# Decoder layer on one core: the third quarter of the output projection for all tokens ahead of the fourth, the triangle matrix kept in another tile, and the slot positions of three token groups taken later

## The chip, the core and the metric

The kernel runs on one core of a Trainium2 chip. A core has five engines with a queue of instructions each: TensorE (PE in the rows: matmuls; PEld its weight loads), VectorE (DVE), ScalarE (ACT), GpSimd (POOL) and SyncE (SP), which here issues every transfer from and to the chip's memory. An engine takes its instructions in the order of its queue and waits at the first one whose inputs or whose place are not ready. The metric is the time of one execution on the device in microseconds (us); less is better.

## What is computed

One layer of a decoder on 512 tokens of 1024 numbers, all in float32 (shapes in the comments):

```python
mixed = sigmoid(ga) * (o_a @ w_proj_a) + sigmoid(gb) * (o_b @ w_proj_b)   # two attention branches
x = x + mixed @ w_out                                                     # [512,1024] @ [1024,1024]
x = x + hier_moe(rms_norm(x, g_ffn), ...)                                 # 32 experts, 2 per token
return rms_norm(x, g_final)

def hier_moe(h, ...):
    g_logit = xt @ w_group + b_group                  # best of 4 groups
    e_logit = (xt @ w_expert + b_expert)              # best 2 of the group's 8 experts
    gate = g_w * top_p / sum(top_p)
    ...
    hid = silu(xb @ w1[e]) * (xb @ w3[e]); return hid @ w2[e]   # 1024 -> 512 -> 1024
```

The change lies between the second line and the first expert: output projection, RMSNorm, choice of experts (routing), and gathering the tokens of each expert.

## The kernel before, in words

The tokens are worked on in NT = 4 groups t of 128. The output projection is cut into four quarters n of 256 columns; `x2_chunk(n, t)` multiplies group t of the merged branches (tile `mt[t]`) with quarter n of the weights (pair `ws[n]`, high and low float32r part) in 24 matmuls (L703 to L705) and adds the result to x on DVE (L707). A table `seq` sets the order of the sixteen chunks. After each, `turn(n, t)` transposes the new columns (PE L733), copies them out of PSUM into the tile `misc` (ACT L736) and sums their squares (ACT L738); for n = 3 that gives the group's scale `rs2` (DVE L744, POOL L745). `logits(n, t)` adds the chunk's share of the routing logits (PE L751).

When a group's four quarters are there, four functions follow for it:

- `route(t)`: some eleven small DVE operations, L758 to L775: logits to `lg`, best group, best two experts, ending in a 0/1 matrix `E[t]`.
- `place(t)`: a matmul of E with the strict triangle `tri` (PE L781; for odd t also L783) counts how many earlier tokens chose the same expert; DVE writes the slot number (`pos`, L784) and the 0/1 gather matrix `sel` (`one_hot`, L826).
- `gates(t)`: eight small DVE operations (L793 to L805) and two on ACT: the gate weights G.
- `h2_parts(t)`: the normalised tokens as float16 high and low parts (tile `h2`): ACT L812 and L817, then a subtraction on POOL (L818) for both halves of the columns; for t = 2 and 3 the second half is subtracted on DVE (L814).

`gather(xs, sel, h, a)` (PE L834, L835; DVE L839) then builds the experts' inputs from h2 and sel: half h = 0 needs groups 0 and 1, h = 1 groups 2 and 3. The experts follow in 8 rounds of 4, each with 24 pieces of weights of 1 MB; `up` and `down` use a piece (PE L886, L893), and `use` gives its place free after the last matmul on it.

Places: SBUF is cut into 22 slots of one piece each (class `Slots`). x2 takes two of them, h2 two, the routing weights with the triangle one (`early`); `mt[t]`, `ws[n]` hold others until they are done. `fetch(n)` takes n free slots and issues the transfer of the next n pieces on SP (L623), which waits there, with everything behind it, until the slot's last user is done. When all that is free, 18 pieces fit; the nineteenth goes out when `use` has freed the first one. For that, five pieces are first multiplied for h = 0 alone (AHEAD = 5), and the first is free after its h = 1 half.

The order of each queue comes from a scheduler at build time, except where `manual_schedule` keeps the order of the code: SP from L691 on, PE and DVE from the last chunk on (`in_order`, in the loop over `seq`), until L1029.

Of the kernel before, what the change touches and what calls it, by code (L numbers as in the profile page):

```python
# [10 lines left out]
F32 = mybir.dt.float32  # L11
# [10 lines left out]
P = 128  # L22
# [10 lines left out]
NL = 40  # L33
# [104 lines left out]
def layer_kernel(ctx: ExitStack, tc: tile.TileContext, xT, x, w_ki, w_ch, w_ab, w_out, g_mix, g_ffnk, g_fin, w_r, b_r,  # L138
# [20 lines left out]
    def t2(shape, dtype=F32, name="t2", tag="r"):  # L159
        return temps[tag][0].tile(shape, dtype, tag=tag, name=name, bufs=temps[tag][1])  # L160
# [451 lines left out]
    def fetch(n):  # L612
        for _ in range(n):
            if not todo or not S.idle:
                return
            if todo[0] == (NQ - 1, PIECES - 4) and not gfn:
                gfn.append(S.get([P, D], F32, "gfn"))
                sp.dma_start(out=gfn[0], in_=g_fin)
                if not S.idle:
                    return  # L620
            q, i = todo.pop(0)
            have[q, i] = S.get([P, QE * FF], F32, "we")
            sp.dma_start(out=have[q, i], in_=w_e[q, i])  # L623
# [9 lines left out]
    br = cp.tile([P, NL], F32, name="br")  # L633
    gfk = cp.tile([P, NK], F32, name="gfk")
    gf8 = cp.tile([P, NK], F32, name="gf8")
    early = S.get([P, NK * NL + P], F32, "early")
    wr, tri = early[:, :NK * NL].rearrange("p (k c) -> p k c", k=NK), early[:, NK * NL:]
    for dst, src in ((br, b_r), (gfk, g_ffnk), (wr, w_r), (tri, const[:, C_COLS["tri"][0]:])):
        sp.dma_start(out=dst, in_=src)
    dve.tensor_scalar(gf8, gfk, 1.0 / H2, None, ALU.mult)  # L640
    merging = ExitStack()
# [48 lines left out]
    S.add(ctx.enter_context(tc.tile_pool(name="more1", bufs=1, side="right", reuse_waits="tile")), N_RIGHT, "m1")  # L690
    ordered = ExitStack()  # L691
    ordered.enter_context(tc.manual_schedule(engines={mybir.EngineType.SP}))
    misc = t2([P, 4 * P], name="misc", tag="y")

    def x2_chunk(n, t, between={}):

        hi, lo = ws[n]
        ps = bank()[:, :CW]
        for k in range(NK):
            for f, *args in between.get(k, ()):  # L700
                f(*args)
            a = mt[t][:, 0, k]
            pe.matmul(ps, a, hi[:, k], start=k == 0, stop=False)  # L703
            pe.matmul(ps, a, lo[:, k], start=False, stop=False)  # L704
            pe.matmul(ps, mt[t][:, 1, k], hi[:, k], start=False, stop=k == NK - 1)  # L705
        o = x2t(t)[:, n * CW:(n + 1) * CW]
        dve.tensor_tensor(o, ps, o, ALU.add)  # L707
# [14 lines left out]
    dve.memset(zero, 0.0)  # L722
    pe.matmul(lps[:, :NT * NL], ident, zero, start=True, stop=False, skip_group_check=True)

    seq = [(n, t) for n in range(2) for t in range(NT)] + [(n, t) for t in range(NT) for n in (2, 3)]
    xts = {}

    def turn(n, t):

        xc = x2t(t)[:, n * CW:(n + 1) * CW]  # L730
        tr = pa.tile([P, 512], F32, tag="sc", name="xtr")
        for k in range(2):
            pe.transpose(tr[:, k * P:(k + 1) * P], xc[:, k * P:(k + 1) * P], ident)  # L733
        a = 2 * P * (seq.index((n, t)) % 2)
        xs = xts[n, t] = misc[:, a:a + 2 * P].rearrange("p (k q) -> p k q", k=2)
        act.copy(xs, tr[:, :CW].rearrange("p (k q) -> p k q", k=2))  # L736
        junk = t2([P, CW], name="junk", tag="hT")
        act.activation(junk, xc, AF.Square, accum_out=ssp[:, t, n:n + 1])  # L738
        if n == 2:
            dve.tensor_reduce(pre[:, t:t + 1], ssp[:, t, 0:3], AX.X, ALU.add)  # L740
            dve.tensor_scalar(pre[:, t:t + 1], pre[:, t:t + 1], 1.0 / (D * H2 * H2), EPS / (H2 * H2), ALU.mult, ALU.add)
        if n == 3:
            r = rs2[:, t:t + 1]
            dve.scalar_tensor_tensor(r, ssp[:, t, 3:4], 1.0 / (D * H2 * H2), pre[:, t:t + 1], ALU.mult, ALU.add)  # L744
            pool.tensor_tensor(r, r, half[:, 0:1], ALU.pow)  # L745
# [102 lines left out]

    sel = t2([P, NT, QE, CAP], F16, name="sel", tag="sel")
    for n, t in seq:  # L850
        if n == 2 and t % 2 == 0:
            h2.append(S.get([P, 2, 2, NK, P], F16, "h2"))
            fetch(len(S.idle))
        if (n, t) == seq[-1]:

            in_order.enter_context(tc.manual_schedule(engines={mybir.EngineType.PE, mybir.EngineType.DVE}))
            x2_chunk(n, t, {3: [(turn, n - 1, t)], 6: [(logits, n - 1, t)]})
        else:
            x2_chunk(n, t)
        if n < 2 and t == NT - 1:  # L860
            S.free(*ws[n])
            fetch(2 - n)
        if n == 3:
            S.free(mt[t])
            if t % 2 == 0:
                fetch(1)
        if (n, t) not in seq[-2:]:
            turn(n, t)
            logits(n, t)
            if n == 3:  # L870
                route(t)
                place(t)
                gates(t)
                h2_parts(t)
        if n == 2 and t == NT - 1:
            S.free(*ws[2])
            fetch(2)
    S.free(*ws[3])
    xs = t2([P, NK, 2, P], name="xs", tag="xs")

# [130 lines left out]

    gather(xs, sel, 0, 0)
    turn(3, NT - 1)
    gather(xs, sel, 0, 4)
    logits(3, NT - 1)
    route(NT - 1)

    h1 = two(pa, "sc", "h1")
    for k in range(AHEAD):
        up(0, k, (0,), h1, xs, have[0, k])  # L1020
        if k == AHEAD - 2:
            h2_parts(NT - 1)
            place(NT - 1)
            S.free(early)
    for a in (0, 4):
        gather(xs, sel, 1, a)
    gates(NT - 1)
    in_order.close()
    fetch(len(S.idle))  # L1029
# [171 lines left out]
```

## Time and profile before

| | |
|---|---|
| time, median of 3 runs | 920.62 us (920.29 to 921.29) |
| profiled execution, its time | 922.1 us |
| its span in the trace | 920.2 us |
| PE busy | 870.4 us (95%) |
| DVE busy | 401.3 us (44%) |
| ACT, POOL busy | 273.2 us (30%), 210.5 us (23%) |
| moved by DMA | 244.50 MB, mean 266 GB/s |
| granted PE clock, mean | 0.994 of full speed |

The span runs from the first to the last instruction in the trace; the time of an execution is 1.9 us longer. Shares are means over stages: the first 440 us or so are attention and projections, the rest the experts. Times in rows count from the span's start. A group's name is its source line, engine and operation; buffer numbers are left out of tile names, so that x2 reads `x`, rs2 `rs`, ev `ev` or `e`.

### The profile page before, as it was taken

Reading aid. Unit: us, or ns where it says so; the run is one execution under the profiler, and the core shown is the slowest. Engines: PE = TensorE matmul, PEld = TensorE weight load, DVE = VectorE, ACT = ScalarE, POOL = GpSimd, SP = SyncE. Lnnn points to the kernel's source line nnn. Section 1 sums busy time; section 2 is a strip of 40 time slices with the busy share of each in tenths; the row PEclk is TensorE's granted clock in tenths of the full one; section 3 lists DMA queues with packets and bytes.
Section 4 is the critical chain, followed back from the end, with each engine's and each line's share of the span. In section 5 each row is a group of like instructions: output and inputs, shape, how many; then the busy total and the mean of one; then the engine's idle time right before and its main releaser. Section 6 shows DMA issues by size and latency. Waiting matters only on the chain.

```text
span 920.2 us, 15647 instructions
## 1 busy us (share of the span) xinstructions
PE 870.4 (95%) x6444; PEld 516.3 (56%) x6444; DVE 401.3 (44%) x957; ACT 273.2 (30%) x582; POOL 210.5 (23%) x135
## 2 busy tenths in 40 slices
PE   7998999999999999999999999999989989989894
PEld 5898779678777877899734243433323214232221
DVE  4736799994444444732814123131311303313113
ACT  5556664562444554534401001010100000101012
POOL 2597445452315831612100000000000000000003
PEclk9999999999999999999999999999999999999998
DMA  9422102112215221682799999999999999999993
GB/s 334 143 70 93 66 27 92 63 53 69 71 69 194 80 92 49 213 360 98 306 410 420 420 421 420 421 419 422 418 421 419 421 420 420 421 419 420 421 403 129
DMA packets 40685, 244.50 MB, mean 266 GB/s; under 512 B 4896, under 2 KB 5280, under 8 KB 16032
## 3 DMA queue, kind: packets, MB, share of 16 engines
q1 hardware_dynamic: 40608, 243.45, 66.5%
q8 instruction: 52, 0.85, 0.4%
q14 instruction: 25, 0.20, 0.1%
HBM read 241.33 MB, written 2.10 MB: 265 GB/s over the span
## 4 chain that ended last, share of the span: by engine, by line
PE 61%; DMA 27%; DVE 6%; POOL 2%; ACT 2%; issue 1%; SPq 0%; POOLq 0%; ACTq 0%
DMA we<-in_w_e_dram 26%; PE h L886 9%; PE y L893 9%; PE mm L264 5%; PE mm L266 5%; PE mm L265 5%; PE ops L475 2%; PE mm L704 2%; PE mm L703 2%; PE mm L705 2%; PE mm L520 2%; PE mm L519 2%; PE mm L518 2%; PE mm L349 2%; PE mm L351 2%; PE mm L350 2%
## 5 line engine op out<-in xcount | busy, mean ns | idle before, releaser
L886 PE MATMUL h<-we,xs 128*32 128x512 f32 x2048 | 237.5, 596 | 20.8 <-DMA we<-in_w_e_dram 20.2
L886 PEld LDWEIGHTS h<-we,xs 128*32 128x32 f32 x2048 | 57.8, 109 | 173.0 <-issue 103.3
L171 POOL TENSOR_TENSOR wl<-raw,wh 128x1024 fp32r<-128x1024 f32 (+1 forms) x41 | 97.1, 2389 | 111.1 <-ACT wh L170 55.6
L893 PE MATMUL y<-we,hT 128*32 128x512 f32 x1024 | 115.4, 595 | 1.6 <-DMA we<-in_w_e_dram 1.4
L264 PE MATMUL mm<-xh,wh 128*128 128x512 f32 (+1 forms) x272 | 109.0, 401 | 0.5 <-DVE bias L408 0.5
L1100 POOL TENSOR_TENSOR fo<-x,gfn 128x512 f32<-128x512 f32 x4 | 5.0, 1287 | 443.4 <-DMA we<-in_w_e_dram 442.6
L266 PE MATMUL mm<-xh,wl 128*128 128x512 f32 (+1 forms) x272 | 106.2, 390 | 0.1
L265 PE MATMUL mm<-xl,wh 128*128 128x512 f32 (+1 forms) x272 | 105.7, 389 | 0.0
L953 DVE TENSOR_TENSOR x<-cps,x 128x512 f32<-128x512 f32 x60 | 41.2, 689 | 91.2 <-PE cps L951 91.0
L893 PEld LDWEIGHTS y<-we,hT 128*32 128x32 f32 x1024 | 30.5, 109 | 71.7 <-issue 59.3
L927 DVE SCALAR_TENSOR_TENSOR silu<-silu,gate,h 128x512 f32<-128x512 f32 x16 | 12.0, 747 | 118.8 <-PE h L886 117.8
L266 PEld LDWEIGHTS mm<-xh,wl 128*128 128x128 f32 x272 | 51.4, 189 | 11.1 <-DVE wl L171 0.6
L264 PEld LDWEIGHTS mm<-xh,wh 128*128 128x128 f32 x272 | 51.5, 189 | 10.0 <-issue 1.0
L170 ACT CAST wh<-raw 128x1024 fp32r<-128x1024 f32 (+1 forms) x46 | 45.6, 1027 | 35.5 <-DMA raw<-in_w_ch_dram 13.2
L265 PEld LDWEIGHTS mm<-xl,wh 128*128 128x128 f32 x272 | 51.6, 190 | 8.0
L934 ACT COPY hT<-htr 128x512 f32<-128x512 f32 x16 | 8.6, 589 | 151.9 <-PE htr L932 151.9
L170 ACT CAST y<-y 128x512 fp32r<-128x512 f32 x30 | 17.6, 586 | 111.5 <-PE y L893 111.5
L921 ACT ACTIVATE silu<-h 128x512 f32<-128x512 f32 x16 | 9.6, 597 | 134.8 <-PE h L886 134.8
L452 ACT ACTIVATE ps<-e,st 128x128 f32<-128x128 f32 (+3 forms) x64 | 33.5, 524 | 50.3 <-DVE st L451 50.2
L171 DVE TENSOR_TENSOR y<-y,y 128x512 fp32r<-128x512 f32 x30 | 20.6, 688 | 53.0 <-ACT y L170 53.0
L705 PE MATMUL mm<-woh,mt 128*128 128x256 f32 x128 | 36.9, 289 | 0.0
L703 PE MATMUL mm<-woh,mt 128*128 128x256 f32 x128 | 36.6, 286 | 0.0
(211 smaller groups left out, 1535.8 us busy)
## 6 DMA issues: line engine op xcount, KB each, us to landing
we<-in_w_e_dram SPq DMA_DIRECT2D x192, 1024.0 KB, 19.8
raw<-in_w_ch_dram SPq DMA_DIRECT2D x44, 512.0 KB, 4.1
raw<-in_w_ab_dram SPq DMA_DIRECT2D x8, 512.0 KB, 3.6
wraw<-in_w_out_dram SPq DMA_DIRECT2D x8, 512.0 KB, 4.4
xraw<-in_xT_dram SPq DMA_DIRECT2D x8, 256.0 KB, 6.0
xtok<-in_x_dram SPq DMA_DIRECT2D x4, 512.0 KB, 9.1
x<-in_x_dram SPq DMA_DIRECT2D x4, 512.0 KB, 6.4
out_dram<-fo SPq DMA_DIRECT2D x4, 512.0 KB, 5.0
```

The costliest lines, as they stand in the source:

```text
L170: act.copy(hi, raw)
L171: eng.tensor_tensor(lo, raw, hi.bitcast(F32), ALU.subtract)
L264: pe.matmul(o, a, xhi, start=k == 0, stop=False)
L265: pe.matmul(o, a, xlo, start=False, stop=False)
L266: pe.matmul(o, lo[:, k, col:col + P], xhi, start=False, stop=k == NK - 1)
L349: pe.matmul(ps, xk(k, 0)[:, sl], hi[:, k], start=k == 0, stop=False)
L452: act.activation(ps[:, :n], e[:, :n], AF.Exp, bias=st[:, 0:1], scale=-1.0, accum_out=st[:, 1:2])
L703: pe.matmul(ps, a, hi[:, k], start=k == 0, stop=False)
L705: pe.matmul(ps, mt[t][:, 1, k], hi[:, k], start=False, stop=k == NK - 1)
L886: pe.matmul(ps[h][CAP * e:CAP * (e + 1)], xs[:, k, h, CAP * e:CAP * (e + 1)], w[:, e * FF:(e + 1) * FF], start=k == 0, stop=k == NK - 1)
L893: pe.matmul(ys[h][CAP * e:CAP * (e + 1)], hT[h][:, k, CAP * e:CAP * (e + 1)], w[:, e * FF:(e + 1) * FF], start=k == 0, stop=k == 3)
L953: dve.tensor_tensor(o, ps, o, ALU.add)
```

## The change

Five edits belong together. The order `seq` runs quarter by quarter for all four quarters (before: quarters 0 and 1 so, then 2 and 3 in turn for each token group). The triangle moves out of `early` into a longer `misc`, and its transfer is issued on SP when misc exists. The float16 places (`h2`) are taken at the fourth quarter, not the third; the slots of `ws[2]` are freed after the third quarter, and one piece is fetched there. In the last chunk `turn` and `logits` of the group before now come with `route` of it, and `h2_parts`, `place` and `gates` of that group stand behind, between the gathers. `early` is freed, and all free slots are fetched, after the last logits (before: after the last place, and the fetch after the last gates).

```diff
-    early = S.get([P, NK * NL + P], F32, "early")
-    wr, tri = early[:, :NK * NL].rearrange("p (k c) -> p k c", k=NK), early[:, NK * NL:]
-    for dst, src in ((br, b_r), (gfk, g_ffnk), (wr, w_r), (tri, const[:, C_COLS["tri"][0]:])):
+    early = S.get([P, NK * NL], F32, "early")
+    wr = early.rearrange("p (k c) -> p k c", k=NK)
+    for dst, src in ((br, b_r), (gfk, g_ffnk), (wr, w_r)):
         sp.dma_start(out=dst, in_=src)
...
-    misc = t2([P, 4 * P], name="misc", tag="y")
+    misc = t2([P, 5 * P], name="misc", tag="y")
+    tri = misc[:, 4 * P:]
+    sp.dma_start(out=tri, in_=const[:, C_COLS["tri"][0]:])
...
-    seq = [(n, t) for n in range(2) for t in range(NT)] + [(n, t) for t in range(NT) for n in (2, 3)]
+    seq = [(n, t) for n in range(4) for t in range(NT)]
...
     for n, t in seq:
-        if n == 2 and t % 2 == 0:
+        if n == 3 and t % 2 == 0:
             h2.append(S.get([P, 2, 2, NK, P], F16, "h2"))
             fetch(len(S.idle))
         if (n, t) == seq[-1]:
 
             in_order.enter_context(tc.manual_schedule(engines={mybir.EngineType.PE, mybir.EngineType.DVE}))
-            x2_chunk(n, t, {3: [(turn, n - 1, t)], 6: [(logits, n - 1, t)]})
+            x2_chunk(n, t, {2: [(turn, n, t - 1)], 4: [(logits, n, t - 1), (route, t - 1)]})
         else:
             x2_chunk(n, t)
-        if n < 2 and t == NT - 1:
+        if n < 3 and t == NT - 1:
             S.free(*ws[n])
-            fetch(2 - n)
+            fetch(2 if n < 2 else 1)
...
-        if n == 2 and t == NT - 1:
-            S.free(*ws[2])
-            fetch(2)
     S.free(*ws[3])
...
     gather(xs, sel, 0, 0)
     turn(3, NT - 1)
+    h2_parts(NT - 2)
     gather(xs, sel, 0, 4)
+    place(NT - 2)
     logits(3, NT - 1)
+    S.free(early)
+    fetch(len(S.idle))
     route(NT - 1)
...
             h2_parts(NT - 1)
             place(NT - 1)
-            S.free(early)
     for a in (0, 4):
         gather(xs, sel, 1, a)
+    gates(NT - 2)
     gates(NT - 1)
```

How this moves instructions is seen in the order of three queues. On **PE**, before, the matmul of `place(0)` (tile `pps`) stands inside the chunk of quarter 3 and token group 2 (`mt_3598`), between two of its matmuls:

```order
L705 MATMUL mm<-woh_3828,mt_3598 128x256
L703 MATMUL mm<-woh_3828,mt_3598 128x256
L704 MATMUL mm<-wol_3829,mt_3598 128x256
L781 MATMUL pps<-E,early_3609 128x32
L705 MATMUL mm<-woh_3828,mt_3598 128x256
L703 MATMUL mm<-woh_3828,mt_3598 128x256
```

In the change it stands behind the last chunk of all (`mt_3599` is token group 3), with those of `place(1)`, and the first gather (`gps`) follows at once:

```order
L706 MATMUL mm<-wol_3828,mt_3599 128x256
L707 MATMUL mm<-woh_3828,mt_3599 128x256
L783 MATMUL pps<-E,misc 128x32 x2
L785 MATMUL pps<-E,cb 128x32
L836 LDWEIGHTS h_64_4299
L836 MATMUL gps<-sel,h_64_4299 128x128
```

Nothing stands any more between the places of groups 0 and 1 and the gather that reads their sel; before, fifteen matmuls of the last chunk, two transposes and four routing matmuls stood between place(1) and it.

On **DVE**, before, the routing of token group 0 runs from its logits `lg` to its matrix `E` with little between, and the add of a later chunk (L707) follows it:

```order
L758 SCALAR_TENSOR_TENSOR lg<-lps,rs_3851,br 128x40
L744 SCALAR_TENSOR_TENSOR rs_3851<-ssp,pre 128x1
L761 MAX gv<-lg 128x8
L762 MAX_INDEX gi<-gv,lg 128x8
L793 TENSOR_SCALAR d_4247<-lg,gv 128x4
L764 TENSOR_SCALAR pen<-cb,gi 128x4
L768 TENSOR_TENSOR lg<-lg,pen 128x32
L770 MAX ev<-lg 128x8
```

In the change the routing of groups 0, 1 and 2 is interleaved there (three `lg<-lps` within nineteen rows; these are the last two):

```order
L760 SCALAR_TENSOR_TENSOR lg<-lps,rs_3851,br 128x40
L775 TENSOR_SCALAR o_4351<-cb,ei 128x32
L805 CAST ef<-ei 128x1
L763 MAX gv<-lg 128x8
L777 SCALAR_TENSOR_TENSOR E<-cb,ei,o_4351 128x32
L764 MAX_INDEX gi<-gv,lg 128x8
L795 TENSOR_SCALAR d_4442<-lg,gv 128x4
L766 TENSOR_SCALAR pen<-cb,gi 128x4
L760 SCALAR_TENSOR_TENSOR lg<-lps,rs_3851,br 128x40
L801 SCALAR_TENSOR_TENSOR g_4366<-e_4363,gs 128x1
```

All of route and place for the four groups now comes after the add of chunk (3, 2), the last but one; before, the first two groups were routed while quarters 2 and 3 of the later groups were still multiplied.

On **SP** the triangle's transfer moves from among the transfers of the output weights (`wraw`) to the head of the expert weights (`we`):

```order
 L193 DMA wraw_3600<-in_w_out_dram 128x1024 x2
-L639 DMA early_3609<-in_const_dram 128x128
 L193 DMA wraw_3603<-in_w_out_dram 128x1024 x2
 L193 DMA wraw<-in_w_out_dram 128x1024 x4
+L695 DMA misc<-in_const_dram 128x128
 L623 DMA we_3858<-in_w_e_dram 128x2048
 L623 DMA we_3860<-in_w_e_dram 128x2048
```

It there waits for the end of the last split of the output weights on DVE, for which the seventh piece of expert weights waited before. The pieces that follow these seven are counted by chunk: before, 9 are issued by the end of quarter 0, 10 by the end of quarter 1, then one each after chunks (3, 0) and (3, 2), two after (2, 3), three after (3, 3), one after place(3); now 9, then 11 by the end of quarter 1, one each after (2, 3), (3, 0) and (3, 2), three after (3, 3), one after the last logits.

## Rows read from the trace of the kernel before

**Rows 1.** The page: span, and GB/s moved by DMA in 40 slices of 23.0 us

```profile
span 920.2 us, 15647 instructions
GB/s 334 143 70 93 66 27 92 63 53 69 71 69 194 80 92 49 213 360 98 306 410 420 420 421 420 421 419 422 418 421 419 421 420 420 421 419 420 421 403 129
```

**Rows 2.** Busy time by stretch; the first row names the columns

```profile
core 0: us, PE busy (x) PEld busy (x) DVE busy (x) ACT busy (x) POOL busy (x), PEclk, DMA share, GB/s
432.70:455.95 23.25, 22.66 (x213) 19.23 (x212) 19.11 (x94) 11.58 (x34) 6.34 (x7) 1.00 0.61 234
448.40:455.95 7.55, 7.41 (x84) 4.11 (x81) 7.14 (x30) 3.02 (x7) 1.71 (x2) 1.00 1.00 399
459.50:480.00 20.50, 20.50 (x192) 6.30 (x188) 3.58 (x12) 2.52 (x4) 0.00 (x0) 1.00 1.00 408
480.00:900.00 420.00, 397.94 (x3472) 134.67 (x3468) 109.17 (x174) 36.49 (x66) 3.10 (x3) 1.00 1.01 418
```

**Rows 3.** Line L623 in four short stretches: issues of weight pieces, time to landing

```profile
L623 SPq DMA_DIRECT2D we<-in_w_e_dram x1: 328/328/328, 392.8 to 392.8; - x1
...
L623 SPq DMA_DIRECT2D we<-in_w_e_dram x2: 327/376/424, 404.7 to 405.1; - x2
...
DMA to landing us min/median/max: 9.4/10.4/11.5
...
L623 SPq DMA_DIRECT2D we<-in_w_e_dram x1: 328/328/328, 459.5 to 459.5; - x1
...
DMA to landing us min/median/max: 6.3/6.3/6.3
...
L623 SPq DMA_DIRECT2D we<-in_w_e_dram x1: 327/327/327, 468.1 to 468.1; - x1
...
DMA to landing us min/median/max: 15.1/15.1/15.1
```

**Rows 4.** Timeline of DVE, 422 to 432.8: start, duration, instruction, idle time before

```profile
422.13 0.42 DVE L707 TENSOR_TENSOR x<-mm,x 128x256 f32<-128x256 f32 x1 [3.06 <-PE mm L705]
...
429.10 0.42 DVE L707 TENSOR_TENSOR x<-mm,x 128x256 f32<-128x256 f32 x1 [2.26 <-PE mm L705]
...
431.98 0.42 DVE L707 TENSOR_TENSOR x<-mm,x 128x256 f32<-128x256 f32 x1 [1.47 <-PE mm L705]
432.77 0.26 DVE L758 SCALAR_TENSOR_TENSOR lg<-lps,rs,br 128x40 f32<-128x40 f32 x1 [0.37 <-PE lps L751]
```

**Rows 5.** Groups of DVE by shape, 432.70 to 455.95: busy us, mean ns, idle before

```profile
L707 DVE TENSOR_TENSOR x<-mm,x 128x256 f32<-128x256 f32 x4 | 1.7, 423 | 1.5 <-PE mm L705 1.5
L804 DVE TENSOR_SCALAR G<-cb,ef,g 128x32 f32<-128x32 f32 x3 | 0.9, 296 | 0.0
L796 DVE TENSOR_TENSOR e<-ev 128x1 f32<-128x1 f32 x3 | 0.4, 141 | 0.0
L740 DVE TENSOR_REDUCE pre<-ssp 128x1 f32<-128x3 f32 x2 | 0.3, 149 | 0.1
```

**Rows 6.** Timeline of DVE, pieces of 437.5 to 456.1

```profile
438.21 0.93 DVE L826 TENSOR_TENSOR sel<-cb,pos 128x128 f16<-128x128 f32 x1
...
443.89 1.07 DVE L814 SCALAR_TENSOR_TENSOR h<-x,rs,h 128x512 f16<-128x512 f32 x1
...
452.51 1.07 DVE L768 TENSOR_TENSOR lg<-lg,pen 128x32 f32<-128x32 f32 x1
...
454.60 0.75 DVE L814 SCALAR_TENSOR_TENSOR h<-x,rs,h 128x512 f16<-128x512 f32 x1
...
455.63 0.29 DVE L826 TENSOR_TENSOR sel<-cb,pos 128x128 f16<-128x128 f32 x1
```

**Rows 7.** Timeline of POOL, 427 to 456: two of six L818

```profile
437.84 1.16 POOL L818 TENSOR_TENSOR h<-f,h 128x512 f16<-128x512 f32 x1 [1.39 <-ACT f L817]
...
452.37 1.17 POOL L818 TENSOR_TENSOR h<-f,h 128x512 f16<-128x512 f32 x1 [1.45 <-ACT f L817]
```

**Rows 8.** Timeline of DVE, 439.2 to 441: routing of token group 1, nothing on POOL

```profile
440.60 0.19 DVE L768 TENSOR_TENSOR lg<-lg,pen 128x32 f32<-128x32 f32 x1
```

## The prediction

> **What bounds the kernel now.** I read the page's slices first, then the stretches, then the issues of the expert weights, then the queues between.
>
> The slices show a kernel in two parts. From the twentieth slice on (about 460 us) DMA moves 410 to 422 GB/s in every slice until the end [rows 1]; between 480 and 900 us its share is 1.01 at 418 GB/s [rows 2]. That part is bound by the weight stream, so the kernel ends when the last piece has come, and a change ahead of it matters by one thing: when the stream starts to run without holes. In the slices of 391 to 460 us it moves 360, 98 and 306 GB/s [rows 1], so there are holes, made by the slots: a piece can go out only when a slot is free.
>
> The issues show where the holes end. Eighteen pieces fit; the nineteenth, for which the first piece must be used up, goes out at 459.5 and lands 6.3 us later; the eighth from there goes out at 468.1 and lands 15.1 later, at 483.2, 23.7 after 459.5 [rows 3]. For comparison I take a burst that started with DMA at rest: first issue at 392.8, its eighth piece issued at 405.1 and landed 11.5 later, 416.6, which is 23.8 after the first [rows 3]. So at 459.5 the stream behaves as if started anew: it had almost run dry, and every us by which that first release comes later is a us at the end, as long as the 18 pieces are in by then. Earlier fetches of the 18 win nothing by themselves, since they only fill places that then stand full.
>
> What sets 459.5? The release needs the first `up` of half 1, this gather(1), this `sel` of group 3. That is the DVE operation at 455.63 (0.29 long) [rows 6]; from its end, 455.9, to the release are 3.6 us of gathers and matmuls. Before it, DVE is busy 7.14 of 7.55 us (448.40 to 455.95), PE 7.41 [rows 2]: both are nearly full, and DVE has the chain route(3), place(3).
>
> **The change part by part.** *Order by quarters, routing later.* Before, the routing of group 0 starts on DVE at 432.77 [rows 4], 23.2 us ahead of the end of sel(3), and DVE is busy 19.11 of these 23.25 us [rows 2]. In the change it starts after chunk (3, 2). I place that by the adds that end a chunk. They come at 422.13 and 429.10 with one between, 3.49 apart; a chunk without transposes and logits in it takes 2.88 (429.10 to 431.98) [rows 4]. After chunk (2, 0) at 422.13, four further chunks with them give 436.1 for (3, 0) and 439.6 for (3, 1); by the order (3, 2) has none in it, so 442.5. The order then puts on PE the same as stood before 432.77 (two transposes, one matmul, the logits): 0.79 after the add [rows 4]. Routing of group 0 starts at 443.3, 10.5 later than before.
>
> What must DVE do from there to sel(3)? What it did in 432.70 to 455.95, less what is now ahead or behind. Ahead: three of four adds (3 of 423 ns, 1.27 us), four operations on `pre` at about 0.149 (0.60), one on rs2 (about 0.15, an estimate by the like-sized rows). Behind: gates of group 2, eight operations of 0.141 to 0.296, about 0.19 each as an estimate, 1.5 [rows 5]. 19.11 - 3.52 = 15.6 us. The idle share I take as in the full stretch, 0.41 in 7.55 [rows 2], so 0.9 in 16.5. Sel(3) ends at 443.3 + 15.6 + 0.9 = 459.8 instead of 455.9: **3.9 us later**, and the release at 463.4. The last chunk on PE is done at about 448 (442.5, 24 matmuls, the transposes and logits of groups 0 to 2 in it); PE then waits, first for sel(1) ahead of gather(0), then for E(3). Behind these waits on PE stand all the experts.
>
> *POOL's subtractions inside the chain.* In the 19.11 us is time in which DVE stood still though it counts as busy: the add of the penalty (L768) took 1.07 us at 452.51, against 0.19 at 440.60 [rows 6, 8], and ended at 453.58 as POOL's L818 ended at 453.54 [rows 7]; sel at 438.21 took 0.93 against 0.29, with POOL at L818 from 437.84 to 439.00; L814 took 1.07 against 0.75 [rows 6]. Together 1.84 us. Four L818 lie between the two ends before; by the order four do so in the change (second group's two, third's and fourth's first), so I leave 1.84 in. Bounds: none of it, 1.84 less; or each of the four holds DVE for nearly its 1.17 us [rows 7], less the operation's own 0.2, 3.9 in place of 1.84, 2.0 more. The Trainium skill, "SBUF — State Buffer", section "SBUF: two separate sides", says that VectorE with two SBUF inputs and GpSimd reading SBUF need one pair of ports, which the first takes for its whole instruction; the trace agrees in these three, and the rule speaks against this change, as DVE's chain has hardly a gap now into which POOL's work falls free. By that rule the sum is the upper bound.
>
> *The fetches.* One piece goes out some 20 us earlier, at the end of quarter 1, and so on; by 443 us 13 instead of 12 are on their way or in. The price is one piece at most, 1.05 MB at 418 GB/s [rows 2], 2.5 us of stream. I take 0: the release, not the count, decides, as shown above. `early` is free after the last logits, about when it was.
>
> *Triangle on SP.* It waits for DVE's last split, and the first two weight pieces are behind it. They would leave some microseconds later, together with the others, ahead of 405. The nine pieces out by 405.1 were in by 416.6 [rows 3]; were all of them to start 12 us later, they would be in by about 429, ahead of the 443 at which more than one follows. Cost 0; without that pause it would be up to 12. *Gates later:* they are wanted by `gsel` for the first `hidden`. After 459.5 DVE is busy 3.58 of 20.50 us [rows 2]; cost 0; without that slack 1.5.
>
> **Sum.** The profiled execution took 922.1 us (span 920.2, 1.9 around it); 922.1 + 3.9 = 926.0. It stands 1.5 above the median of 920.62, so for a median I say 920.6 + 3.9 = **924.5 us**, 0.42% slower. (About 0.2%, 1.8 us, is what a measurement of this kernel can tell from no change.)
>
> **The rivals.** *A, the forecast:* DVE's chain delays sel(3) by 2.4 to 5.3 us: 923.0 to 925.9. *B, DVE held more:* each L818 holds DVE for all its time, +5.9, with twice the idle time +6.8: 926.5 to 927.4. For it: DVE's queue has no gap. Against it: POOL can also fall into operations that take an input from PSUM; all of 19.11 has only 1.84. This is the skill's rule carried through. *C, no change that can be measured:* DVE packs better than in the full stretch (no idle, nothing held): 15.6 - 1.84 = 13.8 us from 443.3, sel(3) at 457.1, +1.2: 921.8. For it: three groups interleaved give each operation something to overlap with, where before one chain waited on itself. Against: the four L818 lie in the chain, and PE's waits for DVE bring DVE waits for PE of their own (places and gathers). That the change does nothing belongs here. *D, faster:* the earlier fetch counts: if the stream never runs dry, the thirteenth piece in at 443 is one piece less to move later, 2.5 us: 918.1. That decides only if the release comes no later than the eighteenth piece is in, at the latest near 459.5, that is, if DVE gets from 443.3 to sel(3) in 12.6 us; below even C.
>
> **How the numbers follow.** A 0.60, B 0.17, C 0.17, D 0.06. A and B are slower by over 0.2%, C is within, D faster. The predicted time is A's. The range leaves out D and the far end of B: 921.2 to 927.2; the bounds of the held time (1.84 less, 2.0 more) lie in it.
>
> **What would show it.** In the changed kernel's trace: the first `lg<-lps` on DVE near 443; DVE busy over nine tenths from there to the `sel` of group 3 near 460; PE idle ahead of the first gather and again ahead of the last place, released by DVE; the nineteenth weight issue near 463.4, with 6.3 us to landing, and DMA at rest shortly before it; from then 418 GB/s as before. The forecast is wrong if that issue stays at 459.5 or earlier, if DMA is still moving the 18 pieces when it comes (then part of the delay is absorbed), or if routing starts well before 443.

## The result, and the profile after

The changed kernel took **928.29 us** (median of 7 runs, 924.27 to 929.70) against 920.78 (7 runs, 920.29 to 921.74) for the kernel before on the same chip: a ratio of 1.006, 95% interval 1.0046 to 1.0074, slower. (The two medians alone would give 1.0082; the ratio on record, here and below, is not theirs.) The profiled execution took 925.28 us (span 923.5), 3.2 more than the one of before. Two later measurements gave 1.006 (1.0043 to 1.0076) and 1.0045 (1.0026 to 1.0064). The executions of the kernel before lie within 1.5 us of each other here, those of the changed one within 5.4. In the later measurements, of 9 to 23 executions, those of the kernel before lie 2.3 to 4.3 us apart, so that the spread alone tells little.

The page's slices of the changed kernel, as in [rows 1]:

```profile
GB/s 321 154 70 93 67 25 92 67 49 69 75 70 197 70 92 64 149 300 266 258 337 421 419 420 420 421 418 421 419 420 419 422 420 420 420 420 420 422 417 145
```

The last two thirds are the same stream as before, 417 to 422 GB/s until the end. The slices ahead of it differ: 149, 300, 266, 258, 337 in place of 213, 360, 98, 306, 410. The hole of 98 is filled, and the stream reaches its full rate one slice later.

Line L623 (the weight pieces) at the nineteenth issue, the first for which a piece must be used up, and at the eighth issue from there:

```profile
L623 SPq DMA_DIRECT2D we<-in_w_e_dram x1: 328/328/328, 464.8 to 464.8; - x1
...
DMA to landing us min/median/max: 5.7/5.7/5.7
...
L623 SPq DMA_DIRECT2D we<-in_w_e_dram x1: 328/328/328, 473.4 to 473.4; - x1
...
DMA to landing us min/median/max: 15.1/15.1/15.1
```

They stood at 459.5 and 468.1, with 15.1 us to the landing of the second too [rows 3]: both come 5.2 to 5.3 us later. Busy time of the changed kernel by stretch, columns as in [rows 2] (the count behind each engine's time, then the granted PE clock, DMA share, GB/s); 443.38 is the start of lg(0) on DVE, 461.15 the end of sel(3):

```profile
443.38:461.15 17.77, 13.51 (x123) 9.95 (x121) 15.87 (x78) 7.18 (x20) 6.13 (x6) 0.90 0.77 296
...
452.10:455.50 3.40, 2.68 (x24) 2.61 (x24) 2.68 (x8) 0.88 (x3) 0.79 (x1) 0.50 1.01 424
...
461.15:464.80 3.65, 3.65 (x53) 2.47 (x50) 1.97 (x7) 0.39 (x3) 0.00 (x0) 1.00 0.02 4
480.00:900.00 420.00, 399.46 (x3496) 134.84 (x3488) 107.43 (x172) 34.74 (x61) 0.14 (x1) 1.00 1.01 420
```

DVE is busy 15.87 of 17.77 us from lg(0) to sel(3). In the 3.65 us behind it, until the release, DMA rests (share 0.02): the last of the 18 pieces has been moved (it counts as landed at 461.7) and no place is free. And for 3.4 us, from 452.1, the granted PE clock is 0.50, the level of 1.2 GHz in place of 2.4.

What PE waits for there, by the queue of waits, 443 to 462 (total us, times, longest):

```profile
PE pps L783 <- DVE E L777: 2.7, 1, 2.7
PE gps L836 <- DVE sel L828: 0.8, 1, 0.8
PE lps L753 <- DVE o L775: 0.8, 1, 0.8
```

The same view of the kernel before, 432.4 to 455.95, has a single row:

```profile
PE lps L751 <- DVE lg L758: 0.4, 1, 0.4
```

So PE, which had been waited for, now waits for DVE: 4.3 us in place of 0.4. What DVE does at that time, in its timeline of the changed kernel (start, duration):

```profile
446.88 1.10 DVE L801 SCALAR_TENSOR_TENSOR g<-e,gs 128x1 f32<-128x1 f32 x1
...
449.31 0.14 DVE L801 SCALAR_TENSOR_TENSOR g<-e,gs 128x1 f32<-128x1 f32 x1
...
449.64 1.23 DVE L777 SCALAR_TENSOR_TENSOR E<-cb,ei,o 128x32 f32<-128x32 f32 x1
...
451.99 0.25 DVE L777 SCALAR_TENSOR_TENSOR E<-cb,ei,o 128x32 f32<-128x32 f32 x1
...
457.65 0.68 DVE L766 TENSOR_SCALAR pen<-cb,gi 128x4 f32<-128x4 f32 x1
```

and POOL in the same stretch:

```profile
446.80 1.17 POOL L820 TENSOR_TENSOR h<-f,h 128x512 f16<-128x512 f32 x1 [1.15 <-ACT f L819]
449.67 1.15 POOL L820 TENSOR_TENSOR h<-f,h 128x512 f16<-128x512 f32 x1 [1.70 <-ACT f L819]
...
457.14 1.17 POOL L820 TENSOR_TENSOR h<-f,h 128x512 f16<-128x512 f32 x1 [1.45 <-ACT f L819]
```

L801 takes 1.10 us in one place and 0.14 in another, L777 1.23 and 0.25; each long one ends with POOL's subtraction (447.98 against 447.97, 450.87 against 450.82, 458.33 against 458.31). The row of the long L777 starts 0.03 us ahead of POOL's, but DVE's operation before it runs until 449.72. The E that took 1.23 is that for which PE waits 2.7.

### The profile page after: what moved, and what is told of

Read it like the earlier page. It is cut to its first block, busy times and chain, and to the rows that moved or that the text cites. A ratio compares the mean times of both kernels' runs of the same rounds, so it can differ in the third digit from the quotient of the medians.

```text
span 923.5 us, 15648 instructions
## 1 busy us (share of the span) xinstructions
PE 871.3 (94%) x6444; PEld 517.3 (56%) x6444; DVE 401.2 (43%) x957; ACT 272.8 (30%) x582; POOL 210.6 (23%) x135
## 4 chain that ended last, share of the span: by engine, by line
PE 67%; DMA 21%; DVE 6%; POOL 2%; ACT 2%; issue 1%; SPq 0%; POOLq 0%; ACTq 0%; DVEq 0%
DMA we<-in_w_e_dram 20%; PE h L885 15%; PE y L892 9%; PE mm L264 5%; PE mm L266 5%; PE mm L265 5%; PE ops L475 2%; PE cps L949 2%; PE mm L520 2%; PE mm L519 2%; PE mm L518 2%; PE mm L705 2%; PE mm L706 2%; PE mm L349 2%; PE mm L707 2%; PE mm L351 2%
## 5 line engine op out<-in xcount | busy, mean ns | idle before, releaser
L707 PE MATMUL mm<-woh,mt 128*128 128x256 f32 x128 | 36.9, 289 | 0.0
```

## The experiments

Four theories were tried. Theory 1 is the forecast's: sel(3) on DVE sets the first release, and the release sets the end. Theory 2: the low clock behind PE's waits is part of the loss. Theory 3: POOL's subtractions hold DVE, and theory 4: only in the change does that cost anything. The rival to all is that another of the five edits costs the time. The traces stand shifted against each other by up to 1.8 us, so sel(3) and the nineteenth issue are compared with the end of an add. In the runs made from the changed kernel it is that of chunk (3, 0), with which token group 0 is complete. In the runs made from the kernel before it is the one that starts at 431.98 [rows 4] and ends at 432.40, the last ahead of lg(0). The recorded expectation of one run calls this one (3, 0) too, but it is (3, 1): in the kernel before, (3, 0) ends at 426.04. Distances from an add are therefore compared only between runs made from the same kernel; where both kernels meet, under "What caused it", an event is used that they share. Each run was timed beside the kernel before.

**The changed kernel twice more.**

> The changed kernel once more, for a second profile and more times. Theory 1 (DVE's chain from lg(0) to sel(3) decides): the stretch repeats, lg(0) at 443.4, sel(3) ends at 461.2, the nineteenth weight issue at 464.8, each within 0.4 us, and a time of 925 to 930 us. Theory 2 (the granted PE clock takes part): the profiled execution shows a stretch at clock 0.5 behind PE's waits near 452, and if the execution is one of the longer ones (its mean clock 0.988 to 0.990 where the first profile has 0.992) at least one further such stretch of about 3.4 us, which the first profile has not. If theory 1 alone holds, the longer executions show a later sel(3) without one.

926.79 us (924.03 to 928.46), ratio 1.006. The profiled execution took 926.9: lg(0) at 443.68, sel(3) at 461.51, the issue at 465.13, the clock at 0.5 from 452.6 to 456.0. The stretch repeats within 0.1 us of its length. The nineteenth piece landed 6.9 us after its issue in place of 5.7; of these 1.25 us 0.95 are left at the last landing, the largest part of the 1.6 us between the two executions.

> The changed kernel a third time, for the profile of one more execution: those of the first two took 925.3 and 926.9 us, others up to 929.7 at a mean clock of 0.988 to 0.990. If this one is longer than 927.5, theory 2 wants a second stretch at clock 0.5 near PE's waits of 445 to 460, with sel(3) or the nineteenth issue more than 0.5 us later than 461.2 and 464.8; the rival, that transfers make the difference, wants sel(3) and the issue in place and the landings of the pieces later (in the second profile the nineteenth landed 6.9 us after its issue, in the first 5.7). If it is shorter, the cause of the longest executions stays open.

925.72 us (923.57 to 929.01), ratio 1.0045. The profiled execution was a long one, 928.45 us. Its stretches:

```profile
448.00:449.40 1.40, 0.00 (x0) 0.00 (x0) 1.40 (x5) 0.24 (x1) 1.08 (x1) 1.00 0.84 263
449.40:459.80 10.40, 9.90 (x64) 6.91 (x68) 7.92 (x34) 2.83 (x6) 2.22 (x3) 0.51 0.86 340
459.80:463.00 3.20, 3.20 (x28) 0.92 (x20) 0.58 (x3) 0.00 (x0) 0.00 (x0) 0.99 0.19 79
```

The clock fell at 449.6, at the end of PE's wait for E(1); in the first profile it fell only in the wait behind that, at 452.1. And it stayed low for some 10 us in place of 3.4, though PE was busy 9.90 of the 10.40 us shown. The matmuls of the experts' first pieces, ahead of the last place, ran at half speed, and sel(3) came 20.7 us after lg(0) in place of 17.8, the issue 24.3 in place of 21.4. These 2.9 us are the largest difference between the two executions, which lie 3.2 apart; there are smaller ones of both signs (lg(0) stood 1.4 us earlier here, the nineteenth piece landed 1.0 later after its issue, and 0.8 us more went by behind the last landing). The executions without a kept trace speak for the same: of the nineteen of the changed kernel, the seven with a mean granted clock of 0.990 or less took 926.66 to 929.70 us (median 928.7), the twelve with 0.992 or more 923.57 to 928.46 (median 925.8). So the low clock goes with the long executions; which stretch of them it lengthened, one profile shows.

**Keep PE busy in its wait.** `spin(n)` ahead of the first gather, and in the first of two trials ahead of the last place too:

```diff
+    def spin(n):
+        ps = bank("spin")
+        for k in range(n):
+            pe.matmul(ps[:, :P], ident, ident, start=k == 0, stop=k == n - 1)
+    spin(14)
     gather(xs, sel, 0, 0)
...
+            spin(8)
             h2_parts(NT - 1)
             place(NT - 1)
```

> The changed kernel with matmuls of no use (identity by identity, 14 ahead of the first gather, where PE stood idle 3.5 us, 8 ahead of the last place), so that PE doesn't rest. Theory 2: the clock stays at 1.0 between 448 and 460, the 32 matmuls of the first gathers go out every 0.055 us in place of 0.107, DVE's two waits for them (0.48 and 0.56) go, sel(3) ends about 1.0 earlier at 460.1, the nineteenth issue at 463.7; time about 1 us below the changed kernel's best and its executions within 2 us of each other, median 924 to 925. Theory 1 alone: the clock is a side effect; sel(3) stays at 461.2 within 0.3 and the time with the same spread as the changed kernel's, 925 to 930.

925.65 us (924.79 to 926.86), ratio 1.0051 (1.0038 to 1.0064). The clock stayed at 1.00, lg(3) came at 455.45, 12.4 behind lg(0) in place of 13.5; but each step of `spin` makes two matmuls of 0.11 us, so the second spin was 1.8 us long and the last place waited for it. With the first spin alone:

> The changed kernel with idle matmuls (identity by identity, 28 of 0.11 us) only where PE stood idle ahead of the first gather. The run before had 16 more ahead of the last place, and these stood in front of the release: lg(3) came at 455.45 in place of 456.88, but the last place waited 1.5 us for them. Theory 2 (the low clock behind PE's wait is part of the loss): lg(3) again 12.4 us behind lg(0) in place of 13.5, sel(3) ends at 459.7 to 460.1, the nineteenth issue at 463.3 to 463.8, time 1 to 1.5 us below the changed kernel. Rival (the matmuls only move the wait): sel(3) at 461 and no change in time.

924.55 us (923.91 to 925.32), ratio **1.0037** (1.0024 to 1.005). From the add of (3, 0) to sel(3), and the stretch in which the clock had been low:

```profile
452.80:456.00 3.20, 3.15 (x40) 2.53 (x43) 2.89 (x8) 1.36 (x5) 0.99 (x1) 1.00 1.02 433
436.72:460.31 23.59, 22.06 (x209) 18.57 (x207) 17.31 (x82) 12.61 (x32) 9.55 (x10) 1.00 0.71 270
```

sel(3) comes 0.84 earlier (0.90 after the add), the issue at 463.93. Theory 2 holds for the release: the low clock costs 0.9 us there in the short case. In time the gain is not clear of the noise: 1.0037 lies below the 1.006, 1.006 and 1.0045 of the changed kernel, but the intervals overlap. Five executions within 1.4 us of each other do not show that the low clock makes the spread either, for those of the kernel without POOL's subtractions (next), whose clock stayed at 1.00 in its profile, lie 4.4 apart.

**Without POOL's subtractions, after and before.** The same edit in both:

```diff
-                f = t2([P, 4, P], name="f", tag="selT")
-                act.activation(f, hv[:, q], AF.Copy, scale=r)
-                pool.tensor_tensor(lo[:, q], f, ho[:, q], ALU.subtract)
+                act.activation(lo[:, q], hv[:, q], AF.Copy, scale=r)
```

> The changed kernel without POOL's six subtractions: ACT writes the scaled tokens into the low part themselves (the low part then holds no remainder, so the experts' inputs are nearly doubled). Theory 3 (POOL's subtractions hold DVE): the operations that took 0.62, 1.10, 1.23, 0.68 and 0.30 us (their kind takes 0.14 to 0.25) fall to that; DVE's busy time from lg(0) to the end of sel(3) goes from 15.87 to about 13.0, sel(3) ends near 458.3, the nineteenth issue near 461.9, time 2.5 to 3 us below the changed kernel. Rival (DVE is as slow without them, for the rows were long for another reason, or PE's waits take the gain): sel(3) at 460.5 or later, time within 1 us of the changed kernel.

922.77 us (921.31 to 925.75), ratio **1.0019** (1.001 to 1.0029). The stretch from the add of (3, 0) to sel(3):

```profile
435.98:457.19 21.21, 19.34 (x181) 15.50 (x179) 14.11 (x83) 12.63 (x32) 2.61 (x4) 1.00 0.69 258
```

and that of the changed kernel:

```profile
436.66:461.15 24.49, 20.23 (x181) 16.67 (x179) 17.18 (x82) 12.61 (x32) 9.55 (x10) 0.93 0.69 261
```

From lg(0) to sel(3) alone:

```profile
443.29:457.19 13.90, 12.03 (x118) 8.19 (x116) 12.94 (x78) 7.11 (x21) 1.52 (x2) 1.00 0.77 305
```

DVE has 3.1 us less to do in the same operations from the add on (L801 takes 0.16 each time, L777 0.25), 2.9 from lg(0) on (12.94 in place of 15.87); the stretch from the add is 3.3 us shorter, PE's wait for E(1) falls from 2.7 to 0.5 us, and with it the low clock is gone. The issue comes at 460.81. Theory 3 holds: the release comes 3.3 us earlier after the add, somewhat more than the 2.5 to 3 expected, since the clock's loss goes too. The kernel stays 0.19% slower than before, clear of noise.

> The kernel before without POOL's six subtractions (ACT writes the scaled tokens into the low part, which holds no remainder then). In the changed kernel this brought the release 4.0 us forward. Theory 4 (before, PE is full from the end of the add of chunk (3, 0) to sel(3), 22.9 of 23.5 us, so time in which POOL holds DVE is hidden; in the change PE has room and DVE's chain decides, so it is not): sel(3) within 0.7 us of 455.9, the nineteenth issue at 458.8 to 459.6, time -1 to +0.3 us against before. Rival (the hold costs as much in both): sel(3) 1.8 us earlier or more, the nineteenth issue at 457.7 or earlier.

921.58 us (920.26 to 924.17), ratio 1.0005 (0.9994 to 1.0016): nothing. The two stretches from the end of the add of (3, 1), first without the subtractions:

```profile
432.32:455.57 23.25, 22.80 (x216) 19.48 (x215) 17.37 (x95) 11.84 (x35) 1.63 (x3) 1.00 0.60 234
```

then the kernel before itself:

```profile
432.40:455.92 23.52, 22.93 (x216) 19.53 (x215) 19.09 (x95) 11.88 (x35) 6.34 (x7) 1.00 0.61 232
```

DVE has 1.7 us less to do, sel(3) comes 0.3 earlier, the issue at 459.19. Before, PE is busy 22.9 of 23.5 us here, so time lost on DVE is hidden behind PE. Theory 4 holds.

**All edits but the order; the gates alone.** In the kernel before: triangle in `misc`, `early` freed and the free slots fetched after the last logits, gates of group 2 behind the gathers (its diff is that of the change without `seq`, `h2` and `ws[2]`); and, in the second kernel, nothing but the gates of all groups moved there.

```diff
-                gates(t)
                 h2_parts(t)
...
-    gates(NT - 1)
+    for t in range(NT):
+        gates(t)
```

> The kernel before with the edits that leave its order of chunks: triangle in misc, its tile free and all free slots fetched after the last logits, gates of group 2 behind the gathers. Theory 1 (the order alone costs): no slower than before; with eight operations of the gates gone from DVE's chain sel(3) ends 0.5 to 1.5 us earlier, at 454.4 to 455.4; the weights that are still on their way at 459.5 (the eighteenth piece lands at 462.7) leave of it at most 0.6 at the end: time -1 to +0.3 us against before. Rival (triangle, gates or fetches cost part of the loss): 1 us or more above before.

920.61 us (918.96 to 923.82), ratio 0.9997 (0.9986 to 1.0008).

> The kernel before with the gates of all groups behind the last gathers (inputs kept in misc), nothing else. Theory 1: DVE's chain is 1.5 us shorter in its full stretch, sel(3) ends 1 to 2 us earlier, near 454 to 455, the nineteenth issue near 458; but the eighteenth piece still lands at 462.7, so the stream has no rest left to fill and the end comes only 0 to 0.6 us earlier, plus what the fetch behind the last place gains by coming earlier: time -1.5 to 0 us against before. If every us at the release were a us at the end on this side too: -1.5 to -2.

921.45 us (919.91 to 923.53), ratio 1.0004 (0.9993 to 1.0015).

The rival falls for these edits: they cost nothing that can be measured. But theory 1's half of it, that sel(3) would come earlier, failed too: 455.92 and 455.56, 23.3 us behind the add in both, in place of 23.5; the issue at 459.54 and 459.18. DVE had 0.5 and 3.2 us less to do in this stretch (18.56 and 15.86 us in place of 19.09) and was hardly earlier, for PE was the bound (22.86 and 22.87 us busy of 23.3). It is the same finding as without the subtractions. The later places for h2 and the slots of `ws[2]` go with the order, and no run tests them by themselves.

**Routing earlier in the quarter order.** The order of PE and DVE is written out from chunk (3, 1) on. First trial, and the mended one:

```diff
+            x2_chunk(n, t, {1: [(place, t - 2)] if t > 1 else [], 2: [(turn, n, t - 1)],
+                            4: [(logits, n, t - 1), (route, t - 1)]})
...
+            x2_chunk(n, t, {2: [(turn, n, t - 1)], 4: [(logits, n, t - 1)], 7: [(place, t - 2)] if t > 1 else []})
+            route(t - 1)
```

> The changed kernel with the order of PE and DVE written out from the chunk (3, 1) on: transposes, logits and routing of group t stand in the chunk (3, t + 1), the place of t in (3, t + 2), gates of 0 and 1 behind the adds. So the quarter order, the slots and the fetches stay, and only the routing starts as soon as it can. Theory 1 (the late start of the routing is the loss): lg(0) comes at 436 to 438.5, sel(3) ends at 455 to 456.5, the nineteenth issue at 458.5 to 460, time 919 to 921.5, no slower than the kernel before. Rival (another of the edits costs, the fetches, the triangle's place or the float16 places taken later): time stays at 924 or more though lg(0) comes early.

927.52 us (926.63 to 928.75), ratio 1.0075 (1.0061 to 1.009). lg(0) came at 438.2 as expected, but sel(3) at 462.5. PE's waits in the stretch:

```profile
PE pps L783 <- DVE E L777: 3.7, 3, 1.4
PE xtr L735 <- DVE x L709: 0.9, 1, 0.9
PE h L885 <- DVE xs L841: 0.7, 1, 0.7
```

Each add stood behind the routing of the group before on DVE, each place on PE waited for that routing, and so the chunks took 5.0, 5.4 and 6.9 us. The clock fell too, behind waits of 0.9 and 1.4 us:

```profile
447.60:451.00 3.40, 3.40 (x18) 3.40 (x17) 2.47 (x15) 1.13 (x3) 0.81 (x2) 0.50 0.27 113
```

> Quarter order, slots and fetches of the change, but routing of group t on DVE right behind the add of chunk (3, t + 1), its place inside chunk (3, t + 2) where E is there, and all gates behind the last gathers (their inputs are kept in misc). In the first trial of an early routing the add of each chunk stood behind the routing on DVE, and PE waited 0.9 to 1.4 us at each place, so the chunks took 5 to 7 us. Theory 1: adds again 3.5 us apart, lg(0) near 439.5, sel(3) ends at 453.5 to 456.5, the nineteenth issue at 457 to 460, time 919 to 921.5, that is no slower than before. Rival (quarter order is slow in itself, by its slots and fetches): 923 or more though sel(3) is early.

925.35 us (924.48 to 926.01), ratio 1.0046 (1.0033 to 1.006). lg(0) at 440.2, and sel(3) still only at 460.41:

```profile
436.29:460.41 24.12, 21.39 (x181) 15.87 (x179) 17.70 (x66) 12.09 (x26) 9.56 (x10) 0.93 0.66 249
```

Two orders with the routing 3 to 5 us earlier take 24.1 and 26.4 us from the first complete group to sel(3), as the change does with 24.5. That the late start of the routing is the loss, which both were meant to show, is not borne out: started earlier, it is spread over the same time. In the mended one POOL's subtractions held DVE about 4.0 us (five operations of 0.78 to 1.22 us, whose kind takes 0.19 to 0.24), and the clock fell:

```profile
454.20:457.60 3.40, 3.40 (x20) 0.87 (x16) 3.23 (x10) 1.95 (x3) 1.96 (x2) 0.50 1.00 417
```

What an early routing would give without these losses of its own stays open.

**Only the release later.** In the kernel before, idle matmuls ahead of gather(1); and memsets ahead of route(3), so that PE has to wait:

```diff
+    spin(19)
     for a in (0, 4):
         gather(xs, sel, 1, a)
```

```diff
+    pause = t2([P, 512], name="pause", tag="y")
+    for _ in range(11):
+        dve.memset(pause, 0.0)
     route(NT - 1)
```

> The kernel before with 38 idle matmuls of 0.111 us (4.2 us in all) ahead of gather(1), so that only the release comes later and PE stays busy. Theory 1 (the end follows the first release): the nineteenth issue goes from 459.5 to 463.7; at 459.5 the last of the 18 pieces were still under way (landed 462.7, the nineteenth 465.8), so about 3.4 of the 4.2 us reach the end: nineteenth landed near 469.2, time +3 to +4 us against before, 924 to 925.5, with executions no further apart than before's. Rival (the release doesn't set the end): time within 1 us of before.

924.04 us (923.30 to 925.17), ratio 1.0031 (1.0019 to 1.0043), that is +2.9 us (1.8 to 4.0). The clock stayed at 1.00, the issue came at 462.94, 4.3 later against the add of (3, 1). By the ratio two thirds of the delay reached the end, in the profiled execution three quarters.

> The kernel before with 11 memsets of 128x512 ahead of route(3) on DVE, about 0.4 us each by the 0.19 of a 128x160 one, so E(3) comes some 4.2 us later and PE stands idle for it ahead of the last place. Theory 2 (PE's idle time ahead of the gathers brings the low clock, and this lengthens the way to the release): clock 0.5 for about 3.4 us somewhere from 456 on, gathers 0.107 apart, and the release later than the wait alone makes it, by up to 1.5 us; executions further apart than those of the busy delay. Rival (an idle PE costs only its idle time): clock 1.0, release later by the length of the memsets.

928.83 us (928.31 to 930.25), ratio 1.0083 (1.007 to 1.0096). The memsets came 0.66 us apart and delayed E(3) by 6.2 us in place of the planned 4.2, PE waited 6.3 us for it, and its clock fell in the wait, at 459.9:

```profile
455.20:460.00 4.80, 0.02 (x4) 0.00 (x0) 3.66 (x12) 0.00 (x0) 0.00 (x0) 0.99 0.71 297
460.00:466.80 6.80, 5.25 (x36) 3.53 (x37) 3.04 (x12) 0.00 (x0) 0.00 (x0) 0.51 0.38 154
466.80:469.00 2.20, 2.20 (x30) 1.24 (x31) 1.59 (x8) 0.63 (x4) 0.00 (x0) 1.00 0.04 7
```

From sel(3) to the release it took 5.57 us (463.16 to 468.73), in place of 3.61 in the kernel before and 3.62 in the changed one. So an idle PE costs 2.0 us beyond its wait here, the expected 1.5 was too little; the spread did not grow.

No version beat the kernel before by more than the measurement can tell; the lowest ratio is 0.9997, of all edits but the order.

## Why the prediction was right, and where its sizes were off

The direction, the path and the place were as forecast: slower, through sel(3) and the first release. The median of 928.29 lies 1.1 us above the range's end; by the ratio, 1.006 of 920.62, the time is 926.1, inside it, 1.6 above the predicted 924.5 and just above the 925.9 at which rival A ends.

- *lg(0) at 443.3*: 443.38. *The edits around the order at 0*: shown together, 0.9997.
- *15.6 us of work on DVE*: 15.87, in part by luck. In it POOL's hold was sized at 1.84; the long rows add up to 2.9 (0.48, 0.95, 0.98, 0.45 of the four longest), and without the subtractions DVE has 2.93 less to do. So the hold was 1.1 too small and the rest, 12.94 in place of 13.8, 0.8 too large. For the kernel before 1.84 was right (1.72 less without the subtractions); there DVE had 4 us of gaps in the stretch.
- *0.9 us idle*: 1.90. The excess is the clock: DVE waits 0.48 and 0.56 for gathers that go out every 0.107 us in place of 0.055; with the spin it is idle 0.87. The forecast had PE idle ahead of the gathers, and did not ask what PE does behind such a wait.
- *sel(3) at 459.8, release at 463.4*: 461.15 and 464.77, both 1.35 late by these two terms. From sel(3) to the release is the same 3.6.
- *Every us at the release is a us at the end*: right within about 1 us. From the nineteenth issue to the landing of the eighth piece from there it takes 23.72 us before and 23.68 after; to the last landing it takes 442.0 to 443.9 in all fourteen traces, whether or not the eighteenth piece was still under way at the release. Before, it was, as this row of the 3.6 us ahead of the release shows (DMA share 0.97; it landed at 462.7):

```profile
455.92:459.53 3.61, 3.61 (x52) 2.47 (x50) 1.97 (x7) 0.38 (x3) 0.00 (x0) 1.00 0.97 377
```

  The two profiled executions lie only 3.2 us apart because the one of before was long: 1.5 above its median, and from the eighth piece to the twenty-second behind the release it took 36.3 us, the other thirteen traces 34.8 to 35.7. So that 925.28 stands near the 926.0 added up for the profiled execution is luck. For a median, 920.6 and the 5.2 us of the release make 925.8, against 926.1 by the ratio.
- *The time of a median from one profile*: the low clock lasts 3.4 us in two profiled executions and some 10 in a third, and this is worth up to 2.9 us at the release. The forecast had no term for it.

**What caused it.** Up to the end of quarter 1 the adds of the two kernels come at the same distances; I count from the end of the last of them, at 419.07 before and 419.24 after. The add that completes token group 0 is known by the operation on rs2 that follows it. Before (DVE):

```profile
425.62 0.42 DVE L707 TENSOR_TENSOR x<-mm,x 128x256 f32<-128x256 f32 x1 [2.08 <-PE mm L705]
426.68 0.16 DVE L744 SCALAR_TENSOR_TENSOR rs<-ssp,pre 128x1 f32<-128x1 f32 x1 [0.64 <-ACT junk L738]
```

and after:

```profile
436.23 0.42 DVE L709 TENSOR_TENSOR x<-mm,x 128x256 f32<-128x256 f32 x1 [2.07 <-PE mm L707]
437.29 0.16 DVE L746 SCALAR_TENSOR_TENSOR rs<-ssp,pre 128x1 f32<-128x1 f32 x1 [0.64 <-ACT junk L740]
```

So the quarter order completes group 0 17.4 us from the common event in place of 7.0. In both kernels lg(0) follows 6.7 us behind, and so it comes 10.4 us later, as forecast. From lg(0) to sel(3) it takes 23.2 us before. These are PE's: it is busy 22.66 of 23.25 us [rows 2], and DVE, held or not, keeps step. After, PE has less left to do there (13.51 us busy), but the stretch shrinks to 17.8 us only, for now DVE's four routings decide it, with all of POOL's hold in the open. Of the 10.4 us some 5.4 are won back, and 5.1 are left at sel(3) and at the release. Hold and clock together make 3.3 of these 5.1, the clock alone 0.9; without both, sel(3) is still 1.8 us later than before.

That the release sets the time is seen in all runs together. How much later than before it came in the profiled execution, from the same common event, and how much longer the kernel took by the ratio, of 921 us:

| run | release, us later | time, us longer |
|---|---|---|
| change without POOL's subtractions | 1.8 | 1.7 |
| change, spin once | 4.2 | 3.4 |
| before, PE busy longer | 4.3 | 2.9 |
| change, routing earlier, mended | 4.7 | 4.2 |
| change, three times | 5.1, 5.1, 8.0 | 5.5, 5.5, 4.1 |
| change, spin twice | 5.5 | 4.7 |
| change, routing earlier, first trial | 7.0 | 6.9 |
| before, PE idle longer | 8.6 | 7.6 |

Times have intervals of 0.9 to 1.8 us to either side, and the 8.0 is of a long execution. This leaves little room for a cost of the slots and fetches beside the release.

Rival B, DVE held for all of each subtraction, was nearer than the forecast's half of it: with 2.9 of an upper bound of 3.9. It was right in the hold and not in the time: its 926.5 to 927.4 lie above the 926.1. The Trainium skill, "SBUF — State Buffer", section "SBUF: two separate sides", gives the rule: whoever has the shared ports first keeps them for its whole instruction. The trace agrees in the three rows above, where DVE ends 0.01 to 0.05 us after POOL, and agrees the other way round: POOL's L747 took 0.98 us at 454.71 in place of 0.54, and ended 0.4 us behind DVE's L816 (454.55 to 455.30).

## What to carry to other kernels

A hold or a slow chain on one engine costs nothing as long as another engine is full in the same stretch: before moving work out of such a stretch, cost what will decide it then, with every hidden stall in the open. Measure from the event that starts the chain (here the first complete group) to the one that ends it, for each engine, and make sure that it is the same event in both traces: adds of different chunks look alike here, and only the operation behind each tells which quarter it ends. If the change leaves TensorE waiting, look at the granted clock behind the wait.

## What the hardware did that was not expected

- A TensorE that had rested 2.7 us, and 0.8 us soon after (busy 1.32 of the 4.1 us from 448.0), went to 1.2 GHz for 3.4 us in two executions; in a third it did so at the end of the 2.7 us, for some 10 us, in which it was busy nearly throughout (9.90 of 10.40). The Trainium skill, "TensorE: Matmul & The Clock Gate", section "Part 1: The HAM clock gate", says that the point of the change varies from run to run, since what the gate looks at does not begin with the kernel. Three executions agree in that: it fell 8.7, 8.9 and 7.6 us behind lg(0). So much variation in length behind one wait was not foreseen. In the two runs with an earlier routing it fell with no wait longer than 1.4 and 1.1 us ahead of it. 28 idle matmuls in the wait kept 2.4 GHz.
- A stream that had come to rest took 4.7 to 6.9 us from its first issue to the landing of the same 1 MB piece in eight traces; the changed kernel alone gave 5.7, 6.7 and 6.9. In the six in which a piece was still under way it took 5.3 to 6.8. What this depends on stays open.
